# First two weight blocks side by side, row squares on ScalarE, chunk inverses by outer products, layer-norm sums kept during the convolution

## The chip, the cores and the metric

One Trainium2 chip, one of its cores, one launch. The metric is the device time of the program in microseconds (us), median of the runs shown. In the rows PE is TensorE's matmul, PEld its weight load, DVE is VectorE, ACT is ScalarE, POOL is GpSimd, SP is SyncE (here it only issues DMAs).

## What is computed

A hybrid layer on x of 256 rows by 4096 columns, all float32. The reference, cut:

```python
h = rms_norm(x, norm_pre_g)                     # x * rsqrt(mean(x*x, -1) + 1e-6) * g
proj = einsum('btd,dc->btc', h, w_in)           # 4096 x 14528 weights
rwkv_in, g_rwkv, glu_v, glu_g, g_conv = split(proj, ...)
xs = rwkv_in + (prev_row(rwkv_in) - rwkv_in) * mu_shift
r, k, v, w_low, a_low = split(xs, ...)          # decay and rate from the two low-rank parts
y = rwkv7_recurrence(r, decay, k_h, v, kk, a)   # 32 heads of 64, 256 steps
y_rwkv = (group_norm(y) * g + b + bonus) * silu(g_rwkv)
u = glu_v * sigmoid(glu_g)
c = causal depthwise conv(u, 31 taps) + conv_b  # 2048 channels
c = silu(layer_norm(c))                         # over the 2048 channels of a row
y_conv = (c @ w_pw2 + b_pw2) * silu(g_conv)
out = concat(y_rwkv, y_conv) @ w_out            # 4096 x 4096
return x + rms_norm(out, norm_post_g)
```

## The kernel before

**Blocks and slots.** The matrix products are cut into 41 blocks: 29 of `w_in` (one for each 512 output columns; the first r block and the low-rank columns make two blocks of 352), 4 of `w_pw2`, 8 of `w_out`. A block has 32 k steps (16 for `w_pw2`) of 128 rows of the weights. A k step is here called a slot; there are 1248. The weights stream from HBM in chunks of two slots (tile `wr`, 4 buffers, 512 KB each for a 512-wide block), issued by SP. Products are made from float32 split into a high and a low part: ScalarE copies `wr` to `wh` (`w_hi`), VectorE subtracts to `wl` (`w_lo`), 5 buffers of each, and a slot is 6 matmuls (`mm`): for each of two halves of 128 rows of x, `wh` by `lh`, `wl` by `lh`, `wh` by `ll` into a PSUM tile `acc` (4 buffers, two for each block). ScalarE's `wh` runs 4 slots ahead of PE, VectorE's `wl` 3.

**The head.** In the first block every slot also splits x: `x_load` fetches a transposed piece of x with the norm's factor as its last column (4 k steps a piece, 514 KB, into tiles `c_ar`, `c_q`, `c_bkt`, `c_uv`), `x_hi` makes `lh` on ScalarE and `x_lo` makes `ll` on VectorE. For the norm, `x_sq` squares each piece on GpSimd and adds it up there (tiles `t_bk`, `c_y`, 15 instructions of 128x1024 in all); `job_rstd` sums over the partitions with 8 small matmuls, takes the root and the reciprocal. Nothing of a block's result is evicted before this `rstd` is there, since the eviction scales by it. The blocks come in the order k, r (352), r rest with low-rank (352), v, gg, gv, then five blocks (k, r, v, gg, gv) for each further quarter of the channels.

**Side work.** Everything else is cut into generators (`job_...`) in lanes. At each slot `side.step` takes one step of each lane, as long as the costs booked for VectorE and ScalarE stay under those of PE; a step that yields 0 may be followed by the next at once. The order on PE, VectorE and ScalarE is that of the program. `job_prep` makes, for 4 heads at a time (8 units), the keys, decays and the masked products `qp` (64 small matmuls in two steps of 32, called `tp<-c_ar,t_bk` in the rows); `job_inv` inverts 32x32 triangular blocks of two units on VectorE (4 times; 31 steps, each a multiply and a reduction, on tiles `t_x`, `c_y`, `c_sq`); `job_chain` runs the recurrence over 8 chunks of 32 rows; `job_conv` makes the 31 taps on VectorE and writes the result to HBM; `job_ln` reads it back (tile `c_c`), sums over channels with five reductions of 128x1024 (line 783), subtracts the mean, squares on ScalarE, sums again with five reductions (line 800), scales, applies SiLU. `job_gate`, `job_mixr`, `job_mixc` build the input of the last product.

All instructions recorded through the helper `Meter` have its line, L90; SP's weight loads are L1107 and L1111.

Of the kernel before, what the change touches and what calls it, by code (L numbers as in the profile page):

```python
# [34 lines left out]
HI_LEAD, LO_LEAD = 4, 3  # L35
MANUAL = {mybir.EngineType.PE, mybir.EngineType.DVE, mybir.EngineType.Activation}
# [139 lines left out]
def hybrid(ctx: ExitStack, tc, a, out):  # L176
# [123 lines left out]

    def x_sq(i):
        xr = st["xr", i][:, :, 0:T]
        if i == 0:
            st["sa"] = rw["pool"].tile([P, 4, T], F32, name="c_y", bufs=1)
            nc.gpsimd.tensor_tensor(out=st["sa"], in0=xr, in1=xr, op=ALU.mult)
        else:
            q = rw["pool"].tile([P, 4, T], F32, name="t_bk", bufs=1)
            nc.gpsimd.tensor_tensor(out=q, in0=xr, in1=xr, op=ALU.mult)
            nc.gpsimd.tensor_tensor(out=st["sa"], in0=st["sa"], in1=q, op=ALU.add)

    def job_rstd():
# [6 lines left out]
        s1 = one.tile([P, 2], F32, name="s1")  # L318
# [109 lines left out]
    def job_prep(u):  # L428
# [112 lines left out]
        for c in range(NCH):  # L541
            for q, h in DIAG:
                pe.matmul(qp[h][HS[q ^ h], c, :], bk[HS[h], c, q, :], ar[HS[h], q * 8 + c, :], start=True, stop=True)
            if c % 4 == 3:
                for q in range(2 if c == 3 else 0):
                    vec.scalar_tensor_tensor(out=bq[:, q * T:(q + 1) * T], in0=rsv[:, q, :], scalar=par("r_k", u * 2 + q),
                                             in1=kh[:, q * T:(q + 1) * T], op0=ALU.mult, op1=ALU.mult)
                yield
# [35 lines left out]
    def job_inv(pr):  # L584
# [14 lines left out]
        vec.memset(nt.rearrange("p n k j -> p n (k j)")[:, :, 0:CH * CH:CH + 1], -1.0)  # L599
        yield 0  # L600
# [138 lines left out]
    def job_conv(j, u):  # L739
        for half in range(2):  # L740
            yield from tp_wait()
            tp = tp_get([P, 2, T])
            transposes(tp, u, half)
            if half:
                pt_put()
            yield
            ups = []
            for q in range(2):
                up = cvp.tile([P, CK - 1 + T], F32, name="up", bufs=3)
                vec.memset(up[:, 0:CK - 1], 0.0)  # L750
                act(out=up[:, CK - 1:], in_=tp[:, q, :], func=AF.Copy)
                ups.append(up)
            tp_put()
            yield
            c0 = j * 4 + half * 2
            c = cvp.tile([P, 2, T], F32, name="cw", bufs=2)
            for q in range(2):
                ct = c0 + q
                vec.tensor_scalar(out=c[:, q, :], in0=ups[q][:, 0:T], scalar1=par("conv_w", ct * CK), scalar2=par("conv_b", ct),
                                  op0=ALU.mult, op1=ALU.add)  # L760
            yield 0
            for k in range(1, CK):
                for q in range(2):
                    ct = c0 + q
                    vec.scalar_tensor_tensor(out=c[:, q, :], in0=ups[q][:, k:k + T], scalar=par("conv_w", ct * CK + k),
                                             in1=c[:, q, :], op0=ALU.mult, op1=ALU.add)
                    yield 0
            nc.gpsimd.dma_start(out=c_dr[j, :, half], in_=c.rearrange("p q t -> p (q t)"))

    def job_ln():  # L770
# [5 lines left out]
        for _ in range(6):  # L776
            yield
        s = cp.tile([P, T], F32, name="ln_s", bufs=1)
        s4 = cp.tile([P, 4, T], F32, name="ln_t", bufs=2)
        for b in range(4):  # L780
            vec.tensor_reduce(out=s4[:, b, :], in_=c[:, 4 * b:4 * b + 4, :].rearrange("p c t -> p t c"), axis=AX.X, op=ALU.add)
            yield 0
        vec.tensor_reduce(out=s, in_=s4.rearrange("p c t -> p t c"), axis=AX.X, op=ALU.add)
        for _ in range(3):
            yield
        yield from tp_wait()
        m = tp_get([P, T])
        pe.matmul(m, cs("mean"), s, start=True, stop=True)
# [8 lines left out]
        for b in range(4):  # L797
# [204 lines left out]
    ss2 = one.tile([P, 2, NB], F32, name="ss2")  # L1002
# [62 lines left out]
    for g in range(4):  # L1065
        for kind in "krv":
# [18 lines left out]
    for bi, b in enumerate(blocks):
        for k0 in range(0, b["nk"], KC):
            for kk in range(KC):
                slots.append((bi, k0 + kk, len(chunks), kk))
            chunks.append((bi, k0))
# [61 lines left out]
    with tc.manual_schedule(engines=MANUAL):  # L1151
# [107 lines left out]
```

## Time and profile before

| | |
|---|---|
| Time, median of 3 runs (lowest, highest) | 1880.1 us (1877.75, 1880.76) |
| The profiled execution: time, span | 1882.28 us, 1880.5 us |
| PE, PEld busy, share of the span | 98%, 80% |
| DVE, ACT, POOL busy | 75%, 54%, 8% |
| granted clock, mean | 0.995 |
| HBM read, written | 348.38 MB, 12.58 MB |
| Chain that ended last, by engine | PE 89%, DVE 7%, issue 2%, ACT 1%, DMA 1% |

The span is the stretch from the program's first instruction to its last; 1.8 us of the time lie around it. Busy time on PE counts matmuls that overlap in the array (one of 512 columns takes 387 to 395 ns, the next starts 227 ns later), so a full row of nines in the slices hides short idle stretches: these are read from the timeline, where each row has in brackets how long its engine was idle before it and what ended that.

### The profile page before, as it was taken

What the parts mean: (1) busy time and instruction counts of PE and PEld (TensorE: products, weight loads), DVE (VectorE), ACT (ScalarE), POOL (GpSimd) and SP (SyncE); (2) the same over time, 40 slices, a digit from 0 to 9 for tenths busy, and PEclk for the clock granted to TensorE, in tenths of its full rate; (3) what the DMA queues carried; (4) which work ended last, traced back from release to release, by engine and by line L of the source; (5) the groups of instructions that cost most, each with busy time, mean ns of one, the idle gap of its engine ahead of it and who ended that gap; (6) DMA issues with size and microseconds to landing.
All of it is one profiled execution on the core that took longest, in us unless ns stands there. A gap on an engine that the chain in (4) does not pass through costs nothing.

```text
span 1880.5 us, 31312 instructions
## 1 busy us (share of the span) xinstructions
PE 1850.0 (98%) x11585; PEld 1497.2 (80%) x11585; DVE 1415.1 (75%) x2623; ACT 1019.1 (54%) x1770; POOL 153.4 (8%) x233
## 2 busy tenths in 40 slices
PE   6999999999999999999999999999999999999997
PEld 4898888877788877888777888777888888888886
DVE  8755769997879997798996989956887655555555
ACT  4555665545565564565464565444566544445553
POOL 5200001020001020001020000110010000000000
PEclk8999999999999999999999999999999999999999
DMA  6676557664657664656664667755766766666665
GB/s 214 182 204 192 175 175 206 188 197 130 188 178 199 192 189 132 196 179 193 184 186 135 198 182 219 215 172 161 254 226 241 262 197 198 198 199 201 193 201 190
DMA packets 192713, 363.02 MB, mean 193 GB/s; under 512 B 14256, under 2 KB 31792, under 8 KB 192304
## 3 DMA queue, kind: packets, MB, share of 16 engines
q1 hardware_dynamic: 181200, 331.12, 58.1%
q0 software_dynamic: 11360, 29.90, 5.3%
q8 instruction: 91, 1.49, 0.3%
q14 instruction: 62, 0.51, 0.1%
HBM read 348.38 MB, written 12.58 MB: 192 GB/s over the span
## 4 chain that ended last, share of the span: by engine, by line
PE 89%; DVE 7%; issue 2%; ACT 1%; DMA 1%; SPq 0%; DVEq 0%; ACTq 0%; POOLq 0%
PE acc L90 82%; PE tp L90 4%; DVE wl L90 3%; PE pz L90 3%; DVE c_sq L90 1%; DVE cw L90 1%; DVE ll L90 1%; ACT wh L90 0%; DVE ln_t L90 0%; DMA wr<-in_w_in 0%; DVE t_x L90 0%; DVE chl L90 0%; DMA t_bk<-in_w_lora_up 0%; DVE c_c L90 0%; ACT L90 0%
## 5 line engine op out<-in xcount | busy, mean ns | idle before, releaser
L90 ACT ACTIVATE wh<-wr 128x512 fp32r<-128x512 f32 (+1 forms) x1243 | 771.0, 624 | 679.9 <-PE acc L90 428.3
L90 DVE TENSOR_TENSOR wl<-wr,wh 128x512 fp32r<-128x512 f32 (+1 forms) x1243 | 847.9, 692 | 292.9 <-ACT wh L90 290.1
L90 PE MATMUL acc<-wl,lh 128*128 128x512 f32 (+1 forms) x2358 | 915.5, 388 | 17.1 <-DVE wl L90 16.8
L90 PE MATMUL acc<-wh,lh 128*128 128x512 f32 (+1 forms) x2358 | 930.9, 395 | 1.5 <-ACT wh L90 1.5
L90 PE MATMUL acc<-wh,ll 128*128 128x512 f32 (+1 forms) x2358 | 913.1, 387 | 0.0
L90 PEld LDWEIGHTS acc<-wl,lh 128*128 128x128 f32 x2358 | 444.0, 188 | 108.3 <-DVE wl L90 27.3
L90 PEld LDWEIGHTS acc<-wh,lh 128*128 128x128 f32 x2358 | 443.6, 188 | 94.3 <-ACT wh L90 2.7
L90 PEld LDWEIGHTS acc<-wh,ll 128*128 128x128 f32 x2358 | 443.8, 188 | 88.9
L90 DVE SCALAR_TENSOR_TENSOR cw<-up,pv,cw 128x256 f32<-128x256 f32 x480 | 217.9, 482 | 6.2 <-DMA c_y<-n_dr 5.3
L90 PE MATMUL acc<-wh,chl 128*128 128x512 f32 x256 | 82.5, 397 | 0.0
L90 DVE TENSOR_TENSOR c_sq<-t_x,c_y 128x4 f32<-128x4 f32 (+30 forms) x124 | 63.7, 514 | 0.1
L556 POOL DMA_DIRECT2D n_dr<-c_q x32 | 18.7, 590 | 528.8 <-DVE c_q L90 483.4
L90 DVE TENSOR_SCALAR c_uv<-pz 32x256 f32<-32x256 f32 x32 | 13.6, 426 | 61.5 <-ACT c_uv L90 61.3
L90 PEld LDWEIGHTS acc<-wh,chl 128*128 128x128 f32 x256 | 48.1, 188 | 11.2
L90 ACT ACT_TABLE_LOAD x39 | 50.0, 1283 | 1.4 <-PEq L1231 0.7
L90 PE MATMUL acc<-wl,chl 128*128 128x512 f32 x128 | 50.5, 395 | 0.0
L90 DVE TENSOR_REDUCE t_x<-c_sq 128x2 f32<-128x4 f32 (+30 forms) x124 | 43.5, 351 | 0.1
L90 ACT ACTIVATE c_ry<-pz 128x256 f32<-128x256 f32 x32 | 12.3, 385 | 45.7 <-PE pz L90 43.2
L618 POOL DMA_DIRECT2D c_x<-x_dr x64 | 34.7, 551 | 16.3 <-DMA x_dr<-t_x 12.5
L90 ACT ACTIVATE pt<-acc,rstd 128x512 f32<-128x512 f32 (+3 forms) x52 | 33.8, 654 | 1.6 <-PE acc L90 1.1
L90 DVE TENSOR_TENSOR c_y<-pz,c_ry 32x256 f32<-32x256 f32 (+1 forms) x48 | 20.4, 424 | 18.4 <-PE pz L90 18.0
L90 PEld LDWEIGHTS pz<-c_uv,c_q 32*64 32x64 f32 (+1 forms) x1024 | 19.7, 124 | 14.4 <-issue 12.5
(173 smaller groups left out, 940.1 us busy)
## 6 DMA issues: line engine op xcount, KB each, us to landing
wr<-in_w_in SPq DMA_DIRECT2D x431, 512.0 KB, 3.7
wr<-in_w_out SPq DMA_DIRECT2D x128, 512.0 KB, 4.6
wr<-in_w_pw SPq DMA_DIRECT2D x32, 512.0 KB, 4.8
wr<-in_w_in SPq DMA_DIRECT2D x16, 352.0 KB, 3.5
c_y<-n_dr POOLq DMA_DIRECT2D x16, 256.0 KB, 7.6
out<-chl SPq DMA_DIRECT2D x16, 256.0 KB, 2.2
wr<-in_w_in SPq DMA_DIRECT2D x16, 192.0 KB, 2.7
wr<-in_w_in SPq DMA_DIRECT2D x16, 160.0 KB, 2.4
```

The costliest lines, as they stand in the source:

```text
L90: return f(*args, **kw)
L556: nc.gpsimd.dma_start(out=n_dr[u, y].rearrange("(h g) k j -> k h g j", h=2), in_=qs[y * CH:(y + 1) * CH, :, 1 - x::2, x * CH:(x + 1) * CH])
L618: nc.gpsimd.dma_start(out=xt[y * CH:(y + 1) * CH, un, h * 4:h * 4 + 4], in_=x_dr[2 * pr + un, y ^ (2 * h), h * 4:h * 4 + 4].rearrange("g i ...
```

## The change

Four edits.

1. **Head.** The first two blocks, now k and v, run side by side: two slots of k, two of v, and so on, up to the last four k steps; those come first for k, then for v. Each piece of x now serves four slots of weights in place of two. `rstd` is needed from the end of k.
2. **Row squares.** x is fetched a second time, row by row (`x_rows`, 8 pieces of 128x1024, 512 KB, by SP), and squared and summed on ScalarE with an accumulating activation (`x_sq`); VectorE adds the 4 parts of a row. The GpSimd instructions and the small matmuls are gone.
3. **Inverses and preparation.** `job_inv` takes 31 outer-product steps (multiply, subtract) in place of 31 steps of multiply and reduce, with the longest row first and fewer elements in all; the -1 on the diagonal is no longer set. `job_prep` issues its 64 `qp` matmuls in one step.
4. **Layer norm.** `job_conv` adds its finished channels into `csum` (15 additions of 128x256); `job_ln` waits 4 steps in place of 6 and starts at the mean; the sum of squares is made by additions of 128x1024 in place of reductions.

```diff
+APART = 4
+X_EVERY = 8
...
+    def x_rows(i):
+        t = rw["pool"].tile([P, D // 4], F32, name=("c_y", "t_bk")[i % 2], bufs=1)
+        nc.sync.dma_start(out=t, in_=xk_v[:, i // 4, (i % 4) * (D // 4):(i % 4 + 1) * (D // 4)])
+        st["xs", i] = t
+
     def x_sq(i):
-        xr = st["xr", i][:, :, 0:T]
-        if i == 0:
-            st["sa"] = rw["pool"].tile([P, 4, T], F32, name="c_y", bufs=1)
-            nc.gpsimd.tensor_tensor(out=st["sa"], in0=xr, in1=xr, op=ALU.mult)
-        else:
-            q = rw["pool"].tile([P, 4, T], F32, name="t_bk", bufs=1)
-            nc.gpsimd.tensor_tensor(out=q, in0=xr, in1=xr, op=ALU.mult)
-            nc.gpsimd.tensor_tensor(out=st["sa"], in0=st["sa"], in1=q, op=ALU.add)
+        t = st["xs", i]
+        act(out=t, in_=t, func=AF.Square, accum_out=ss2[:, i // 4, i % 4:i % 4 + 1])
 
     def job_rstd():
-        yield from tp_wait()
-        s = tp_get([P, 2, 2])
-        for tt in range(2):
-            for j in range(4):
-                pe.matmul(s[:, tt, :], st["sa"][:, j, tt * P:(tt + 1) * P], cs("mean")[:, 0:2], start=(j == 0), stop=(j == 3))
-        yield
         s1 = one.tile([P, 2], F32, name="s1")
-        act(out=s1, in_=s[:, :, 0], func=AF.Sqrt, scale=W / D, bias=eps[:, 0:1])
-        tp_put()
+        vec.tensor_reduce(out=s1, in_=ss2[:, :, 0:4], axis=AX.X, op=ALU.add)
+        yield
+        act(out=s1, in_=s1, func=AF.Sqrt, scale=1.0 / D, bias=eps[:, 0:1])
         yield
...
-            if c % 4 == 3:
-                for q in range(2 if c == 3 else 0):
-                    vec.scalar_tensor_tensor(out=bq[:, q * T:(q + 1) * T], ...)
-                yield
+        for q in range(2):
+            vec.scalar_tensor_tensor(out=bq[:, q * T:(q + 1) * T], ...)
+        yield
...
-        for j in range(1, CH):
-            l = (j + 3) // 4 if j % 4 == 0 else j // 4 + 1
+        for k in range(CH - 1):
+
+            l, m = k // 4 + 1, CH - 1 - k
             tm = rp.tile([P, 2, 8, CH], F32, name="c_sq", bufs=1)
-            vec.tensor_tensor(out=tm[:, :, 0:l, 0:j + 1], in0=xi[:, :, 0:l, 0:j + 1],
-                              in1=nt[:, :, 0:j + 1, j].unsqueeze(2).broadcast_to([P, 2, l, j + 1]), op=ALU.mult)
+            vec.tensor_tensor(out=tm[:, :, 0:l, 0:m], in0=xi[:, :, 0:l, k:k + 1].broadcast_to([P, 2, l, m]),
+                              in1=nt[:, :, k:k + 1, k + 1:].broadcast_to([P, 2, l, m]), op=ALU.mult)
             yield 0
-            vec.tensor_reduce(out=xi[:, :, 0:l, j], in_=tm[:, :, 0:l, 0:j + 1], axis=AX.X, op=ALU.add, negate=True)
+            vec.tensor_tensor(out=xi[:, :, 0:l, k + 1:], in0=xi[:, :, 0:l, k + 1:], in1=tm[:, :, 0:l, 0:m], op=ALU.subtract)
             yield 0
...
+            if c0 == 0:
+                vec.tensor_tensor(out=csum, in0=c[:, 0, :], in1=c[:, 1, :], op=ALU.add)
+            else:
+                for q in range(2):
+                    vec.tensor_tensor(out=csum, in0=csum, in1=c[:, q, :], op=ALU.add)
...
-        for kind in "krv":
+        for kind in "kvr" if g == 0 else "krv":
...
+    head = [(bi, k0) for k0 in range(0, NK - APART, KC) for bi in range(2)]
+    head += [(bi, k0) for bi in range(2) for k0 in range(NK - APART, NK, KC)]
...
-        x_load(1)
         load(2)
         load(3)
-        x_load(2)
+        x_load(1)
         load(4)
...
-                if s < 28 and s % 4 == 0:
-                    x_load(s // 4 + 3) if s // 4 + 3 < 8 else None
+                if s % X_EVERY == 0 and s // X_EVERY + 2 < 8:
+                    x_load(s // X_EVERY + 2)
                 load(i + RL)
-            if bi == 0 and k % 4 == 2 and k > 2:
-                x_sq(k // 4)
+            if s % 6 == 0 and 1 <= s // 6 <= 8:
+                x_rows(s // 6 - 1)
+            if s % 6 == 5 and 2 <= s // 6 <= 9:
+                x_sq(s // 6 - 2)
...
-            if bi == 1 and k >= 4:
+            if bi == 2:
                 side.drain(lambda: "rstd" not in st)
             side.step()
-            if evict is not None and (bi != 1 or "rstd" in st):
+            if evict is not None and "rstd" in st:
```

The order of instructions that results, at three places. GpSimd's queue at the start, before; `c_y` and `t_bk` hold the squares, `c_ar` to `c_uv` the pieces of x:

```order
L590 DMA t_x<-in_cst 128x512
L305 ISA
L305 TENSOR_TENSOR c_y<-c_ar 128x1024
L308 TENSOR_TENSOR t_bk<-c_ar 128x1024
L309 TENSOR_TENSOR c_y<-c_y,t_bk 128x1024
L308 TENSOR_TENSOR t_bk<-c_q 128x1024
L309 TENSOR_TENSOR c_y<-c_y,t_bk 128x1024
```

and now:

```order
L1236 UNCONDITIONAL_BRANCH
L588 DMA t_x<-in_cst 128x512
L430 DMA t_bk<-in_w_lora_up 96x256
L431 DMA t_bk<-in_a_lora_up 96x256
L554 DMA n_dr<-c_q 32x8x32 x4
```

All 15 arithmetic instructions have left GpSimd; only DMA issues stay on it.

ScalarE at the end of the first statistics, before (`s` is the root of the mean square, `wh` of 352 columns belongs to the r block):

```order
L90 ACTIVATE wh<-wr 128x512
L90 ACTIVATE wh<-wr 128x352 x4
L90 ACTIVATE s_626<-tp,eps 128x2
L90 ACTIVATE wh<-wr 128x352
L90 ACTIVATE pt<-acc,rstd 128x512
```

and now:

```order
L92 ACTIVATE wh<-wr 128x512 x4
L92 ACTIVATE t_bk,ss_94<-t_bk 128x1024
L92 ACTIVATE wh<-wr 128x512
L92 ACTIVATE s_919<-s_919,eps 128x2
L92 ACTIVATE wh<-wr 128x352
L92 ACTIVATE pt<-acc,rstd 128x512
L92 ACTIVATE wh<-wr 128x352
L92 ACTIVATE pt<-acc,rstd 128x512
```

The last row square, the root and the two evictions of the first block now stand between the last `wh` of the second block and the first ones of the r block, where the root stood behind four of the r block's `wh`.

PE in the preparation of the first unit, before (`acc` rows belong to a block of weights):

```order
L90 MATMUL acc<-wh,ll 128x512
L90 MATMUL tp<-c_ar,t_bk 64x64 x16
L90 MATMUL acc<-wh,lh 128x512
L90 MATMUL acc<-wl,lh 128x512
L90 MATMUL acc<-wh,ll 128x512
L90 MATMUL acc<-wh,lh 128x512
L90 MATMUL acc<-wl,lh 128x512
L90 MATMUL acc<-wh,ll 128x512
L90 MATMUL tp<-c_ar,t_bk 64x64 x16
```

and now:

```order
L92 MATMUL acc<-wl,lh 128x512
L92 MATMUL acc<-wh,ll 128x512
L92 MATMUL tp<-c_ar,t_bk 64x64 x32
L92 MATMUL acc<-wh,lh 128x512
L92 MATMUL acc<-wl,lh 128x512
```

Two pieces with one slot between them have become one piece (a program row of 16 is 32 matmul rows of the trace, since a float32 matmul runs in two passes).

## Rows read from the trace of the kernel before

**Rows 1.** Busy time by stretch: us, then PE, PEld, DVE, ACT, POOL (instructions), PEclk, DMA share, GB/s.

```profile
0.00:26.00 26.00, 14.28 (x40) 7.35 (x40) 19.58 (x16) 12.08 (x23) 17.00 (x12) 0.87 0.64 212
26.00:75.00 49.00, 41.82 (x172) 33.55 (x173) 43.78 (x57) 24.29 (x47) 19.95 (x10) 0.93 0.65 208
75.00:200.00 125.00, 125.00 (x686) 114.36 (x686) 69.58 (x128) 73.39 (x140) 0.00 (x0) 1.00 0.65 188
```

**Rows 2.** Waits of PE from 75 to 1875 us: total us, times, longest.

```profile
PE acc L90 <- DVE wl L90: 0.6, 2, 0.5
```

**Rows 3.** Chain that ended last: start us, us, what.

```profile
153.22 35.41 PE acc L90 x156
```

**Rows 4.** Timeline of PE, 10 to 76 us: start us, us, what [idle before <-releaser].

```profile
10.46 0.51 PE L90 MATMUL acc<-wh,lh 128*128 128x512 f32 x1
...
16.56 0.50 PE L90 MATMUL acc<-wl,lh 128*128 128x512 f32 x1 [3.16 <-DVE wl L90]
...
41.75 0.79 PE L90 MATMUL acc<-wl,lh 128*128 128x512 f32 x1 [3.12 <-DVE wl L90]
...
57.38 0.50 PE L90 MATMUL acc<-wl,lh 128*128 128x512 f32 x1 [2.88 <-DVE wl L90]
...
73.88 1.84 PE L90 MATMUL tp<-cst,c_y 128*128 128x2 f32 x16
75.58 0.41 PE L90 MATMUL acc<-wh,lh 128*128 128x352 f32 x1
```

**Rows 5.** Timeline of DVE, 28 to 37 us.

```profile
28.01 0.47 DVE L90 SCALAR_TENSOR_TENSOR ll<-c_q,lh 128x256 fp32r<-128x256 f32 x1
28.40 0.68 DVE L90 TENSOR_TENSOR wl<-wr,wh 128x512 fp32r<-128x512 f32 x1
...
32.00 2.11 DVE L90 SCALAR_TENSOR_TENSOR ll<-c_q,lh 128x256 fp32r<-128x256 f32 x1
34.03 2.88 DVE L90 TENSOR_TENSOR wl<-wr,wh 128x512 fp32r<-128x512 f32 x1
```

**Rows 6.** Timeline of POOL, 23 to 34 us.

```profile
23.12 2.41 POOL L309 TENSOR_TENSOR c_y<-c_y,t_bk 128x1024 f32<-128x1024 f32 x1
...
31.50 2.33 POOL L308 TENSOR_TENSOR t_bk<-c_bkt 128x1024 f32<-128x1024 f32 x1 [5.97 <-DMA c_bkt<-in_xT]
```

**Rows 7.** DMA from 1.5 to 16.5 us: rate in 40 slices; one issue group, us to landing.

```profile
GB/s 36 200 208 180 371 281 303 334 320 342 296 274 331 336 336 361 320 282 342 345 378 413 396 402 407 388 404 377 375 356 356 364 361 391 372 364 372 351 329 192
...
c_q<-in_xT SPq DMA_DIRECT2D x2, 514.0 KB, 9.5
```

**Rows 8.** Waits of SP's DMA queue, 0 to 75 us.

```profile
SPq L1111 <- DVE ll L90: 40.9, 10, 9.6
```

**Rows 9.** Timeline of PE around two pieces of preparation work.

```profile
230.56 0.39 PE L90 MATMUL acc<-wh,ll 128*128 128x512 f32 x1
...
231.50 0.50 PE L90 MATMUL acc<-wh,lh 128*128 128x512 f32 x1
...
242.27 0.39 PE L90 MATMUL acc<-wh,ll 128*128 128x512 f32 x1
...
243.68 0.50 PE L90 MATMUL acc<-wh,lh 128*128 128x512 f32 x1
```

**Rows 10.** Groups: xcount | busy us, mean ns of one | idle before.

```profile
L90 DVE TENSOR_TENSOR c_sq<-t_x,c_y 128x4 f32<-128x4 f32 (+30 forms) x124 | 63.7, 514 | 0.1
...
L90 DVE TENSOR_REDUCE t_x<-c_sq 128x2 f32<-128x4 f32 (+30 forms) x124 | 43.5, 351 | 0.1
...
L90 ACT ACTIVATE pt<-acc,rstd 128x512 f32<-128x512 f32 (+3 forms) x52 | 33.8, 654 | 1.6 <-PE acc L90 1.1
...
L90 ACT ACTIVATE ln_q<-c_c 128x1024 f32<-128x1024 f32 x4 | 4.2, 1058 | 2.7 <-DVE ln_t L90 2.7
...
L90 ACT ACTIVATION_READ_ACCUMULATOR tp<-acc 128x1 f32 x16 | 3.0, 189 | 0.0
```

**Rows 11.** Tile c_c: landing of its DMA issues.

```profile
DMA to landing us min/median/max: 7.3/9.8/11.7
```

More of the change, by code (lines that the diff above doesn't have):

```diff
@@ L213, in hybrid @@
     rstd = one.tile([P, 2], F32, name="rstd")
+    ss2 = one.tile([P, 2, D // BN], F32, name="ss2")
     lowh = one.tile([LORA, 2, T], F32R, name="lowh")
@@ L216, in hybrid @@
     bones = one.tile([P, P], F32R, name="bones")
+    csum = one.tile([P, T], F32, name="csum")
     ident = cs("ident")
@@ L299, in x_lo @@
                                  in1=st["lh"][:, kt, :].bitcast(F32), op0=ALU.mult, op1=ALU.subtract)
+    def x_rows(i):
+        t = rw["pool"].tile([P, D // 4], F32, name=("c_y", "t_bk")[i % 2], bufs=1)
+        nc.sync.dma_start(out=t, in_=xk_v[:, i // 4, (i % 4) * (D // 4):(i % 4 + 1) * (D // 4)])
+        st["xs", i] = t
     def x_sq(i):
-        xr = st["xr", i][:, :, 0:T]
-        if i == 0:
-            st["sa"] = rw["pool"].tile([P, 4, T], F32, name="c_y", bufs=1)
-            nc.gpsimd.tensor_tensor(out=st["sa"], in0=xr, in1=xr, op=ALU.mult)
-        else:
-            q = rw["pool"].tile([P, 4, T], F32, name="t_bk", bufs=1)
-            nc.gpsimd.tensor_tensor(out=q, in0=xr, in1=xr, op=ALU.mult)
-            nc.gpsimd.tensor_tensor(out=st["sa"], in0=st["sa"], in1=q, op=ALU.add)
-    def job_rstd():
-        yield from tp_wait()
-        s = tp_get([P, 2, 2])
-        for tt in range(2):
-            for j in range(4):
-                pe.matmul(s[:, tt, :], st["sa"][:, j, tt * P:(tt + 1) * P], cs("mean")[:, 0:2], start=(j == 0), stop=(j == 3))
+        t = st["xs", i]
+        act(out=t, in_=t, func=AF.Square, accum_out=ss2[:, i // 4, i % 4:i % 4 + 1])
+    def job_rstd():
+        s1 = one.tile([P, 2], F32, name="s1")
+        vec.tensor_reduce(out=s1, in_=ss2[:, :, 0:4], axis=AX.X, op=ALU.add)
         yield
-        s1 = one.tile([P, 2], F32, name="s1")
-        act(out=s1, in_=s[:, :, 0], func=AF.Sqrt, scale=W / D, bias=eps[:, 0:1])
-        tp_put()
+        act(out=s1, in_=s1, func=AF.Sqrt, scale=1.0 / D, bias=eps[:, 0:1])
         yield
@@ L775, in job_ln @@
             nc.gpsimd.dma_start(out=c[:, 4 * b:4 * b + 4, :].rearrange("p c t -> p (c t)"), in_=c_dr[b].rearrange("p h x -> p (h x)"))
-        for _ in range(6):
-            yield
[L778 to L784, printed above, removed]
+        for _ in range(4):
             yield
@@ L787, in job_ln @@
         m = tp_get([P, T])
-        pe.matmul(m, cs("mean"), s, start=True, stop=True)
+        pe.matmul(m, cs("mean"), csum, start=True, stop=True)
         yield
@@ L796, in job_ln @@
         s4 = cp.tile([P, 4, T], F32, name="ln_t", bufs=2)
-        for b in range(4):
+        act(out=s4, in_=c[:, 0:4, :], func=AF.Square)
+        for b in range(1, 4):
             sq = cp.tile([P, 4, T], F32, name="ln_q", bufs=1)
@@ L800, in job_ln @@
             yield
-            vec.tensor_reduce(out=s4[:, b, :], in_=sq.rearrange("p c t -> p t c"), axis=AX.X, op=ALU.add)
+            vec.tensor_tensor(out=s4, in0=s4, in1=sq, op=ALU.add)
             yield
         cv["sq"] = True
-        vec.tensor_reduce(out=s, in_=s4.rearrange("p c t -> p t c"), axis=AX.X, op=ALU.add)
-        for _ in range(3):
+        vec.tensor_tensor(out=s4[:, 0:2, :], in0=s4[:, 0:2, :], in1=s4[:, 2:4, :], op=ALU.add)
+        vec.tensor_tensor(out=csum, in0=s4[:, 0, :], in1=s4[:, 1, :], op=ALU.add)
+        for _ in range(2):
             yield
@@ L808, in job_ln @@
         m = tp_get([P, T])
-        pe.matmul(m, cs("mean"), s, start=True, stop=True)
+        pe.matmul(m, cs("mean"), csum, start=True, stop=True)
         yield
@@ L1001, in hybrid @@
     NB = D // BN
-    ss2 = one.tile([P, 2, NB], F32, name="ss2")
     def pre_out(j):
@@ L1084, in hybrid @@
     slots = []
[L1085 to L1089, printed above, removed]
+    head = [(bi, k0) for k0 in range(0, NK - APART, KC) for bi in range(2)]
+    head += [(bi, k0) for bi in range(2) for k0 in range(NK - APART, NK, KC)]
+    for bi, k0 in head + [(bi, k0) for bi, b in enumerate(blocks[2:], 2) for k0 in range(0, b["nk"], KC)]:
+        for kk in range(KC):
+            slots.append((bi, k0 + kk, len(chunks), kk))
+        chunks.append((bi, k0))
     st["lh"] = xp.tile([P, NK, T], F32R, name="lh")
@@ L1171, in hybrid @@
                 w_lo(s - (HL - LL))
-        x_sq(0)
         acc = None
@@ L1190, in hybrid @@
                     b["pre"]()
-                acc = [ps_acc.tile([P, b["n"]], F32, name="acc") for _ in range(2)]
+                b["acc"] = [ps_acc.tile([P, b["n"]], F32, name="acc") for _ in range(2)]
+            acc = b["acc"]
             if b["lhs"] is CHL:
@@ L1214, in hybrid @@
                 if evict is not None:
+                    side.drain(lambda: "rstd" not in st)
                     while next(evict, "end") != "end":
```

6 lines of the change are left out of this document (2 added, 4 removed).

## The prediction

> **What bounds the kernel.** I began with busy time by stretch [rows 1]. From 75 us on PE's busy time fills the stretch at a granted clock of 1.00 (the upper level, 2.4 GHz); before that it does not: 14.3 of the first 26 us and 41.8 of the next 49, with the clock at 0.87 and 0.93. Next the waits of PE: from 75 to 1875 us it lost 0.6 us to VectorE's `wl` [rows 2]. So behind the first block only fewer or shorter instructions on PE can change the time, and VectorE, however busy, costs nothing there. The chain gives PE's undisturbed pace: 156 matmuls, which are 26 slots, in 35.41 us, so 1.362 us a slot [rows 3].
>
> The timeline of the head shows what the first block loses. Slot 2 starts at 10.46 us; then PE stands still for about 3 us at a time, at 16.56, 41.75 and 57.38 us among others, each time for VectorE's `wl`; a row of 0.79 us is a matmul at the lower clock (1.2 GHz) behind such a stop. The 16 matmuls of the row statistics follow at 73.88, and the second block starts at 75.58 us [rows 4]. At full pace its 30 slots from 10.46 would have ended at 51.3, so some 24 us are lost. VectorE's own timeline says why: the same `ll` takes 0.47 us at 28.01 and 2.11 at 32.00, the same `wl` 0.68 and 2.88 [rows 5]. The long ones lie where GpSimd computes its squares: its sum at 23.12 ends at 25.53, the next square starts at 31.50 [rows 6], and VectorE is fast in between. Busy time agrees: GpSimd worked 17.0 us of the first 26 and 20.0 of the next 49, and not at all from 75 to 200 [rows 1]. A slow pair (2.11 and 2.88, some overlap) needs about 4.9 us where PE needs 1.36, so VectorE sets the pace while GpSimd computes.
>
> **The change, part by part, against the profiled execution (span 1880.5, time 1882.3, which is 2.2 above the median of 1880.1; I carry the difference over to the median).**
>
> *Head.* To compare like with like I take the end of two 512-wide blocks. Before: 75.58 plus 32 slots of 1.362 (43.6) is 119.2; this holds the old row-statistics matmuls, which are removed. After: the DMAs up to slot 2 stand in the same order, so slot 2 starts at 10.46 again; its `wl` can be ready only about 0.68 after `wh` [rows 5] where the first matmul takes 0.23, a stop of 0.4; then 62 slots of 1.362 (84.4) end at 95.3. That needs VectorE at 0.47 for every second slot and 0.68 for each, 0.9 a slot, which fits. Gain **23.9 us**. Without GpSimd's share a single block would have gained nearly as much; side by side each piece of x serves twice the matmuls.
>
> *What must keep up.* ScalarE gets 8 squares: 1.06 us for 128x1024 and 0.19 for reading the accumulator [rows 10], 10 us in 87, beside some 0.9 us of copies a slot. A square stands 11 slots (15 us) behind its DMA's issue; the slowest landing of a half-megabyte piece of x in the crowded start was 9.5 us [rows 7]. I take 0; each microsecond by which a square came late would be one for every `wh` behind it on ScalarE. SP issues 8 more DMAs among the weight loads; one whose tile is free holds the queue for about half a microsecond, and in the old head that queue stood 40.9 us behind `ll` [rows 8], so it has room. `rstd` now comes after the last square; then the root and two evictions of 0.65 [rows 10], under 3 us, must be done before the r block takes their `acc` tiles. The last four slots of v, 5.4 us of PE, cover it. Without this cover PE would stand up to 3 us.
>
> *DMA.* Between slots 0 and 49 SP issues 25 weight chunks, 6 pieces of x, 8 row pieces and 0.76 MB of parameters: 13.1 + 3.2 + 4.2 + 0.8 = 21.2 MB, in 49 slots or 66.7 us, so 318 GB/s. In the second half of the stretch from 1.5 to 16.5 us, with the queue full, 19 slices of 20 lie between 329 and 413 [rows 7]. The other end: 188 GB/s at a share of 0.65 [rows 1] is 290 GB/s at 1.00; there the 21.2 MB take 73.1 us, 6.4 more than PE, less what the four buffers hold. I take 0, since the full-queue row is the same traffic at the same place, and keep +6 for the range. The Trainium skill (DMA: Bandwidth & Descriptors, Specifications) gives about 358 GB/s for one core's share of HBM: by it the 21.2 MB would take 59 us and cost nothing, while the full-queue slices go above that figure.
>
> *Preparation.* A piece of 32 rows of small matmuls costs PE 0.94 us from the matmul before to the one behind (230.56 to 231.50), one of 64 costs 1.41 (242.27 to 243.68) [rows 9]. Two of the first less the 0.23 that the further matmul would take anyway are 1.65, against 1.41, and the high-part matmul behind every piece itself runs 0.1 longer: 0.35 saved in each of 8 units, **2.8 us**. The two VectorE products that stood between the halves are done elsewhere in its slack.
>
> *Inverses.* Now 107.2 us of VectorE for 124 multiplies and 124 reductions [rows 10]. After: 124 multiplies and 124 subtractions on about half the elements (3120 against 5856 for each pair of units); at most twice the old 63.7, so between 60 less and 20 more on VectorE. PE waited 0.6 us for it in 1800; 0 on PE, with that 0.6 as the most it can give. If the cover went, it would show as `wl` late beside the inverses.
>
> *Layer norm.* Ten reductions of 128x1024 go; 15 additions of 128x256 in the convolution and five larger ones come. All on VectorE under PE: 0. One wait is new: the mean's subtraction follows the reading of `c_c` by five slots (6.8 us), and that lands after 7.3 to 11.7 us [rows 11]. VectorE may stand up to 4.9 us; its lead of three slots (4.1 us) hides all but 0.8. I take 0.
>
> Sum: 23.9 + 2.8 = 26.7 less, a span of 1853.8, a time of 1855.6; on the median 1880.1 - 26.7 = **1853.4 us**.
>
> **Rivals.** *DMA just short, or the clock down for a while.* If the head moves 290 GB/s it loses up to 6.4; a fall of the clock like those behind the old stops, for 4 to 8 us of PE's work, costs 2 to 4. For it: 318 needed is close to what the queue has shown. Against: the full-queue slices. Time about 1859, up to 1866.
>
> *The slow VectorE rows are not GpSimd's doing* but go with the landing of x itself. Then the head keeps its stops and only the small pieces (2.8) and the old row-statistics matmuls (1.7, from 73.88 to 75.58 [rows 4]) are gained: 1875.6. Against it: long and short rows part exactly at GpSimd's start and end.
>
> *The squares hold ScalarE.* If the row pieces land two microseconds after their square's turn, eight times, 16 of the gain go: 1869. For it: they queue behind weights in a DMA system near its limit. Against: 15 us of lead.
>
> *Slower.* The head becomes bound by DMA altogether. Its first 26 us moved 212 GB/s [rows 1]; were that what the chip gives to this traffic, 21.2 MB would take 100 us, 33 more than PE: the head would end at 128.6 in place of 119.2, and with the 2.8 the time is 1886.7. It decides from where the head ends at 122.0, a rate of 227 GB/s. Against it: in that stretch the queue was waiting for buffers that VectorE freed late [rows 8], not for the transfers.
>
> **How the numbers follow.** Forecast as summed, 1849 to 1858: 0.69. DMA or clock, 1857 to 1866: 0.17. Slow rows stay: 0.05. Squares hold ScalarE: 0.05. Slower: 0.04. The range 1848 to 1866 takes the first two. 0.2% (3.8 us) is about what a measurement of this kernel can tell from no change; the rivals that gain lie below that bound, so faster 0.95, same 0.01, slower 0.04.
>
> **What would show it.** Right: GpSimd has no arithmetic; VectorE's `ll` and `wl` stay near 0.47 and 0.68 from the start; no stop of PE over half a microsecond between 12 and 95 us; the r block's first matmul near 95; a clock above 0.95 in the first 75 us; 8 pieces of 64 rows near 1.4 us; PE's time from the r block on unchanged but for these. Wrong: stops of PE that end with a DMA of `wr`, `ll` near 2 us without GpSimd, squares that start on a landing, a first r matmul after 100 us, or `wl` late behind `c_c`.

## The result and the profile after

The changed kernel takes **1850.25 us**, the median of 4 runs (1849.65 to 1850.36), against 1879.57 for the kernel before on the same chip: a ratio of 0.984, 95% interval 0.983 to 0.986, or 29.3 us less. The forecast was 1853.4, which is 26.7 less than the 1880.1 it started from. In the three later sets of runs the kernel before took 1877.56 to 1878.72, so by the set the gain is 27.3 to 29.3. The profiled execution took 1850.36 us with a span of 1848.5.

The page of the changed kernel, its first part (busy time, share, instructions) and the first line of the chain by engine:

```profile
PE 1835.3 (99%) x11569; PEld 1495.3 (81%) x11569; DVE 1345.9 (73%) x2630; ACT 1024.4 (55%) x1785; POOL 118.3 (6%) x218
...
PE 98%; DVE 1%; DMA 0%; ACT 0%; SPq 0%; issue 0%; DVEq 0%
```

Busy time by stretch in the changed kernel, with the columns of [rows 1]:

```profile
0.00:26.00 26.00, 23.38 (x88) 16.38 (x89) 14.95 (x31) 15.67 (x29) 0.87 (x5) 1.00 0.95 329
26.00:75.00 49.00, 49.00 (x218) 40.57 (x217) 32.59 (x59) 35.76 (x68) 0.00 (x0) 1.00 0.93 319
75.00:200.00 125.00, 125.00 (x685) 114.39 (x684) 72.48 (x134) 81.75 (x157) 1.04 (x2) 1.00 0.67 189
```

PE now fills the second stretch (49.00 of 49.00), the granted clock is 1.00, the upper level, from the start, and GpSimd computes nothing any more (the 0.87 us are four memsets and a DMA issue). The price is in the last two columns: the DMA share of the head went from 0.64 to 0.95.

PE's timeline in the changed kernel: slot 2, the first 352-wide matmul (the r block) and the first matmul of the fifth block (slot 128).

```profile
10.23 0.50 PE L92 MATMUL acc<-wh,lh 128*128 128x512 f32 x1 [0.92 <-ACT wh L92]
10.96 0.49 PE L92 MATMUL acc<-wl,lh 128*128 128x512 f32 x1 [0.23 <-DVE wl L92]
...
95.20 0.32 PE L92 MATMUL acc<-wh,lh 128*128 128x352 f32 x1
...
158.41 0.39 PE L92 MATMUL acc<-wh,lh 128*128 128x512 f32 x1
```

The same place in the kernel before, and below it, for each kernel, the first matmul of slot 928, where the product with `w_pw2` begins. First before:

```profile
183.03 0.39 PE L90 MATMUL acc<-wh,lh 128*128 128x512 f32 x1
...
1427.43 0.40 PE L90 MATMUL acc<-wh,chl 128*128 128x512 f32 x1
```

and after:

```profile
1395.71 0.40 PE L92 MATMUL acc<-wh,chl 128*128 128x512 f32 x1
```

This places the gain. After 128 slots, the same work in both orders, the changed kernel is 183.03 - 158.41 = 24.6 us ahead. From slot 128 to 928 it gains 31.7 - 24.6 = 7.1 more, and from there to the end only 0.3 (the spans differ by 32.0). So there are two gains: the head, and the middle (slots 128 to 928), where the chunk preparation, the inverses and the layer norm run under PE. Both are differences between one execution of each kernel; the part on the prediction says how much of them belongs to the execution.

VectorE's timeline in the head reads like the fast pair of [rows 5] now, though x arrives at the same time:

```profile
23.98 0.69 DVE L92 TENSOR_TENSOR wl<-wr,wh 128x512 fp32r<-128x512 f32 x1 [0.67 <-ACT wh L92]
24.59 0.47 DVE L92 SCALAR_TENSOR_TENSOR ll<-c_q,lh 128x256 fp32r<-128x256 f32 x1
```

The groups of the inverses, and of the mean's subtraction behind `c_c`, against [rows 10]:

```profile
L92 DVE TENSOR_TENSOR c_sq<-t_x,c_y 128x120 f32<-128x120 f32 (+24 forms) x124 | 31.8, 257 | 4.0 <-DMA c_y<-n_dr 3.9
L92 DVE TENSOR_TENSOR t_x<-t_x,c_sq 128x120 f32<-128x120 f32 (+24 forms) x124 | 31.7, 256 | 0.1
...
L92 DVE TENSOR_TENSOR c_c<-c_c,tp 128x1024 f32<-128x1024 f32 x4 | 4.8, 1214 | 1.8 <-DMA c_c<-c_dr 1.8
```

The inverses take 63.5 us of VectorE instead of 107.2. The new wait behind `c_c` exists: VectorE stood 1.8 us for that DMA.

### The profile page after: what moved, and what is told of

It is laid out like the page before. It is cut to its first block, busy times and chain, and to the rows that moved or that the text cites. A ratio compares the mean times of both kernels' runs of the same rounds, so it can differ in the third digit from the quotient of the medians.

```text
span 1848.5 us, 31244 instructions
## 1 busy us (share of the span) xinstructions
PE 1835.3 (99%) x11569; PEld 1495.3 (81%) x11569; DVE 1345.9 (73%) x2630; ACT 1024.4 (55%) x1785; POOL 118.3 (6%) x218
## 4 chain that ended last, share of the span: by engine, by line
PE 98%; DVE 1%; DMA 0%; ACT 0%; SPq 0%; issue 0%; DVEq 0%
PE acc L92 92%; PE tp L92 4%; PE pz L92 3%; DMA wr<-in_w_in 0%; DVE chl L92 0%; DVE wl L92 0%; DVE t_pi L92 0%; ACT L92 0%; SPq L291 0%; ACT wh L92 0%; DVE c_y L92 0%; SPq L1104 0%; ACT tp L92 0%; DVEq L1236 0%; ACT t_sw L92 0%
## 5 line engine op out<-in xcount | busy, mean ns | idle before, releaser
L92 DVE TENSOR_TENSOR wl<-wr,wh 128x512 fp32r<-128x512 f32 (+1 forms) x1243 | 831.5, 677 | 339.9 <-ACT wh L92 335.4
L92 PEld LDWEIGHTS acc<-wh,chl 128*128 128x128 f32 x256 | 48.1, 188 | 11.1
L554 POOL DMA_DIRECT2D n_dr<-c_q x32 | 18.6, 589 | 489.0 <-DVE c_q L92 438.3
L92 DVE TENSOR_TENSOR c_sq<-t_x,c_y 128x120 f32<-128x120 f32 (+24 forms) x124 | 31.8, 257 | 4.0 <-DMA c_y<-n_dr 3.9
L92 DVE TENSOR_TENSOR t_x<-t_x,c_sq 128x120 f32<-128x120 f32 (+24 forms) x124 | 31.7, 256 | 0.1
L92 DVE RECIPROCAL t<-t 128x128 f32<-128x128 f32 x32 | 29.8, 940 | 0.3
```

Of the source, the lines that this page charges most:

```text
L92: return f(*args, **kw)
L554: nc.gpsimd.dma_start(out=n_dr[u, y].rearrange("(h g) k j -> k h g j", h=2), in_=qs[y * CH:(y + 1) * CH, :, 1 - x::2, x * CH:(x + 1) * CH])
```

## Experiments

All kernels were timed beside the kernel before, whose median was 1877.56 in the first set (7 runs), 1878.72 in the second (7) and 1878.04 in the third (21). The changed kernel was timed again in the second set: 1850.04 (1849.59 to 1850.54). A loss is counted from 1850.25 in the first set and from 1850.04 in the second.

**The head: which part gives the 24 us?** My theory was that GpSimd's squares slow VectorE; the rivals were a loss that comes with x's landing, a DMA limit, and squares that hold ScalarE.

*Squares alone moved, blocks still one after the other* (on the kernel before):

```diff
 def x_sq(i):
-    xr = st["xr", i][:, :, 0:T]
...
-        nc.gpsimd.tensor_tensor(out=q, in0=xr, in1=xr, op=ALU.mult)
-        nc.gpsimd.tensor_tensor(out=st["sa"], in0=st["sa"], in1=q, op=ALU.add)
+    act(out=t, in_=t, func=AF.Square, accum_out=ss2[:, i // 4, i % 4:i % 4 + 1])
...
+            if s % 3 == 0 and s // 3 < 8:
+                x_rows(s // 3)
+            if s % 3 == 2 and 2 <= s // 3 <= 9:
+                x_sq(s // 3 - 2)
```

> The kernel before with one edit: x read a second time by rows and its squares made on ScalarE (8 pieces, one every 3 slots), nothing of them on GpSimd; blocks one after the other, as before. If the head was lost to GpSimd's arithmetic alone, VectorE's ll and wl stay at 0.47 and 0.68 and the second block starts near 52 in place of 75.6 us: about 1857. If the second reading of x needs the blocks side by side to be carried, the first block is bound by DMA: 8.4 MB of weights, 8.4 of x and some 2.5 run ahead in one block at 320 to 370 GB/s take 52 to 60 us, so the second block starts at 58 to 66: 1863 to 1871, with stops of PE that end with a DMA. If VectorE is slowed by the landing of x, its rows stay at 2 to 2.9 us and the time stays near 1875.

Measured: 1858.99 (1858.63 to 1859.22), ratio 0.990 [0.988, 0.991]; 18.6 us from this part alone, where the whole change gives 27.3 against this set's kernel before. Its stretches, then its second block and its slot 128:

```profile
0.00:26.00 26.00, 23.40 (x89) 15.99 (x90) 15.64 (x33) 16.87 (x33) 0.87 (x5) 1.00 0.97 340
26.00:75.00 49.00, 48.22 (x249) 41.79 (x248) 33.07 (x69) 38.23 (x82) 1.04 (x2) 1.00 0.89 298
```

```profile
53.90 0.32 PE L90 MATMUL acc<-wh,lh 128*128 128x352 f32 x1
...
161.26 0.39 PE L90 MATMUL acc<-wh,lh 128*128 128x512 f32 x1
```

The second block starts at 53.90 instead of 75.58 [rows 4], at a DMA share of 0.97, and PE is busy 48.22 of the 49 us. So even one block after the other the transfers carried the head.

*The GpSimd instructions put back into the changed kernel, their result unused:*

```diff
+    def idle_sq(i):
+        xr = st["xr", i][:, :, 0:T]
+        q = rw["pool"].tile([P, 4, T], F32, name="c_bv", bufs=1)
+        nc.gpsimd.tensor_tensor(out=q, in0=xr, in1=xr, op=ALU.mult)
+        if i:
+            nc.gpsimd.tensor_tensor(out=q, in0=q, in1=xr, op=ALU.add)
...
+            if s % 8 == 2 and s // 8 < 8:
+                idle_sq(s // 8)
```

> The changed kernel with the 15 GpSimd instructions of 128x1024 put back in the head, their result used by nobody. If GpSimd's arithmetic is what slows VectorE, ll and wl beside them take 2.1 and 2.8 us again, PE stops for about 3 us at a time and 15 to 22 us of the gain are lost: 1865 to 1872. If VectorE's slow rows came from the landing of x, nothing changes: 1850.

Measured: 1856.50 (1854.14 to 1857.65), ratio 0.988 [0.987, 0.990]; 6.3 us lost, well under the 15 to 22 that I had written down. The profiled execution is the fastest of the four: 1854.14, 3.8 above that of the changed kernel. Timelines of its GpSimd, VectorE and PE:

```profile
16.39 2.26 POOL L320 TENSOR_TENSOR c_bv<-c_bv,c_ar 128x1024 f32<-128x1024 f32 x1
18.73 2.23 POOL L318 TENSOR_TENSOR c_bv<-c_q 128x1024 f32<-128x1024 f32 x1
21.03 2.23 POOL L320 TENSOR_TENSOR c_bv<-c_bv,c_q 128x1024 f32<-128x1024 f32 x1
30.93 1.89 POOL L318 TENSOR_TENSOR c_bv<-c_q 128x1024 f32<-128x1024 f32 x1 [7.67 <-DMA c_q<-in_xT]
32.90 2.19 POOL L320 TENSOR_TENSOR c_bv<-c_bv,c_q 128x1024 f32<-128x1024 f32 x1
```

```profile
16.51 2.69 DVE L92 TENSOR_TENSOR wl<-wr,wh 128x512 fp32r<-128x512 f32 x1
19.12 2.11 DVE L92 SCALAR_TENSOR_TENSOR ll<-c_ar,lh 128x256 fp32r<-128x256 f32 x1
```

```profile
23.87 0.50 PE L92 MATMUL acc<-wl,lh 128*128 128x512 f32 x1 [2.94 <-DVE wl L92]
```

The long `ll` and `wl` are back, in the changed kernel, with data that nobody reads. That is the cause; x's landing is not. What I had mis-sized is when it costs: the first burst has four instructions without a gap (13.72 to 23.26) and ends in one stop of PE, 2.94 us. The later ones have two (30.93 to 35.09, 4.2 us), and no stop follows: PE is busy 49.00 us of the stretch from 26 to 75. That VectorE catches up in between, since side by side it needs 0.9 of every 1.36 us, is argued. The other three executions lost 5.9 to 7.4 us at a mean granted clock of 0.997 in place of 0.998; no trace shows where.

*The old statistics on GpSimd whole, blocks side by side* (the changed kernel with the old `x_sq` and `job_rstd`, and in the loop):

```diff
-            if s % 6 == 0 and 1 <= s // 6 <= 8:
-                x_rows(s // 6 - 1)
-            if s % 6 == 5 and 2 <= s // 6 <= 9:
-                x_sq(s // 6 - 2)
+            if s % 8 == 2 and s // 8 < 8:
+                x_sq(s // 8)
```

> The changed kernel with the old row statistics: squares and sums on GpSimd from the transposed pieces, no second reading, the blocks still side by side. If GpSimd's arithmetic is the cause, 36 us of it in the head cost about as much as before, spread over two blocks: ll and wl at 2.1 and 2.8 us beside it, 15 to 24 us lost, 1865 to 1875. If placing the blocks side by side is what gained, by halving what VectorE must do for x in a slot, it stays within 5 us of 1850.

Measured: 1863.08 (1861.34 to 1866.37), ratio 0.992 [0.991, 0.994]; 12.8 us lost, under the 15 to 24 expected. PE's waits in the first 100 us (total, times, longest), and its slot 128:

```profile
PE acc L92 <- DVE wl L92: 8.3, 8, 3.1
```

```profile
171.90 0.39 PE L92 MATMUL acc<-wh,lh 128*128 128x512 f32 x1
```

Here GpSimd computes almost without a gap from 52.09 to 67.7 us, and stops of PE come back there. Slot 128 starts 13.5 us later than in the changed kernel: 8.3 are these waits, the old row-statistics matmuls (1.7) stand in the head again, and the granted clock is 0.97 and 0.94 in the stretches to 26 and 75 us. With this run the head is a table of four starts of slot 128: 183.0 as it was; 171.9 with only the blocks side by side; 161.3 with only the squares moved; 158.4 with both. Moving the squares gives 21.8 alone, going side by side 11.1 alone, and only 2.9 once the squares are gone. Each start is that of one execution, and the one of the kernel before was long in its head: in two other runs with the same head (new inverses alone and one-step qp alone, below) slot 128 starts at 180.21 and 180.72, by which the first two gains are 2.3 to 2.8 smaller.

*Changed kernel without the second reading of x and the squares:*

```diff
-            if s % 6 == 0 and 1 <= s // 6 <= 8:
-                x_rows(s // 6 - 1)
-            if s % 6 == 5 and 2 <= s // 6 <= 9:
-                x_sq(s // 6 - 2)
+            if s == 5:
+                vec.memset(ss2[:, :, 0:4], 1024.0)
```

> The changed kernel without the row statistics (the sums of squares are constants; neither the second reading of x nor the 8 squares are done). If the second reading costs nothing since PE is the bound in the head, the first r matmul stays at 95.2 us and the time at 1850 within 0.7. If DMA at a share of 0.93 to 0.95 holds PE back somewhere, or ScalarE does, up to 1.5 us are gained.

Measured: 1851.49 (1850.70 to 1852.40), ratio 0.986 [0.984, 0.988]: no gain, and 1.2 us above the changed kernel where I had allowed 0.7. The r block begins at 95.91 instead of 95.20, but slot 2 at 10.97 instead of 10.23: between the two lie 84.94 us here and 84.97 in the changed kernel. The 4.2 MB read again and 10 us of ScalarE cost nothing, as I took them.

**The middle: where do 7 us come from, when I had 2.8?** Each of the three edits was undone in the changed kernel, and two were done alone on the kernel before; the layer norm alone was not run. Beside the time I read each run's middle, from the start of slot 128 to that of slot 928. In four executions with the changed kernel's order there (two of the changed kernel, the idle GpSimd instructions, the old statistics) it is 1237.3 to 1237.4 us.

*Old inverses in the changed kernel* (the memset and the loop of 15 multiplies and reductions in place of the outer products):

```diff
+        vec.memset(nt.rearrange("p n k j -> p n (k j)")[:, :, 0:CH * CH:CH + 1], -1.0)
...
+            vec.tensor_reduce(out=xi[:, :, 0:l, j], in_=tm[:, :, 0:l, 0:j + 1], axis=AX.X, op=ALU.add, negate=True)
-            vec.tensor_tensor(out=xi[:, :, 0:l, k + 1:], in0=xi[:, :, 0:l, k + 1:], in1=tm[:, :, 0:l, 0:m], op=ALU.subtract)
```

> The changed kernel with the old inverses (multiply and reduce). From slot 128 to slot 928 the change gained 7.1 us where I had 2.8; the rest lies in rows of PE in which the first low-part matmul came late. If the old inverses held wl up (107 us of VectorE in place of 63.5), 3 to 4 us are lost: 1853 to 1854, with wl among the waits of the weight load again. If the gain came from fewer pieces of small matmuls alone, it loses under 1 us (203 pieces in place of 200).

Measured: 1854.87 (1853.95 to 1856.53), ratio 0.987 [0.986, 0.989]; 4.8 us lost; the middle is 1241.5, 4.2 longer. The waits behind the head tell where, once the weight-load engine is looked at beside PE. Its row in the kernel before, and in this run:

```profile
PEld acc L90 <- DVE wl L90: 7.0, 19, 0.9
```

```profile
PEld acc L92 <- DVE wl L92: 6.2, 18, 1.0
```

The changed kernel has no such row in that stretch. PE's own row in the kernel before showed 0.6 [rows 2]; the `wl` that is late holds up its weight load first, and the time is booked there. Of the 18 waits of this run 17 lie at its fourth inverse (1119 to 1176 us). Of the 19 of the kernel before ten (3.0 us) lie at the third inverse, six (2.1) at the fourth and three (1.9) beside the old layer norm's reductions, so 5.1 of the 7.0 us belong to the inverses.

What such a wait costs can be read from the first experiment (squares alone moved). Behind the head its PE, VectorE and ScalarE have the instructions of the kernel before in the same order, yet its middle is 1404.09 - 161.26 = 1242.8 us, where the kernel before has 1427.43 - 183.03 = 1244.4. The two keep step within 0.2 us up to slot 565; then the third inverse begins. The kernel before from 860 to 945 us, its weight load and the VectorE row ahead of that inverse:

```profile
PEld acc L90 <- DVE wl L90: 3.0, 10, 0.5
```

```profile
866.60 0.44 DVE L90 SCALAR_TENSOR_TENSOR cw<-up,pv,cw 128x256 f32<-128x256 f32 x1 [3.73 <-DMA c_y<-n_dr]
```

and in the first experiment the same VectorE row, and its slot 928:

```profile
841.48 0.44 DVE L90 SCALAR_TENSOR_TENSOR cw<-up,pv,cw 128x256 f32<-128x256 f32 x1 [0.24 <-DVE wl L90]
```

```profile
1404.09 0.40 PE L90 MATMUL acc<-wh,chl 128*128 128x512 f32 x1
```

There the weight load has none of the ten waits. So 3.0 us of them cost PE 1.6, while PE's own row for `wl` in the middle is 0.6 us in the kernel before and 0.7 in the experiment. They came after VectorE had stood 3.73 us for the landing of the triangular blocks (`c_y<-n_dr`); that this landing used up its lead is read from this one pair. With the new inverses VectorE stood 3.9 to 7.0 us for the same landing in the four executions named above, whose middles agree within 0.1 us.

*The qp products in two steps again:*

```diff
+            if c % 4 == 3:
+                for q in range(2 if c == 3 else 0):
...
+                yield
```

> The changed kernel with the masked products in two steps of 32 again. By the prediction 0.35 us in each of 8 units: 2.8 lost, 1853.1. By the count of pieces (205 in place of 200, since other pieces meet) at 0.25 to 0.35 each, 1.3 to 1.8: 1851.8. If pieces cost nothing, 1850.3.

Measured: 1853.87 (1853.69 to 1854.10), ratio 0.987 [0.985, 0.988]; 3.8 us lost, against 1.3 to 2.8 expected; the middle is 1241.2, 3.9 longer. PE's pieces of small matmuls behave as read: one of 64 in the changed kernel takes 217.42 to 218.83, the 1.41 of [rows 9].

```profile
217.42 0.39 PE L92 MATMUL acc<-wh,ll 128*128 128x512 f32 x1
217.74 1.16 PE L92 MATMUL tp<-c_ar,t_bk 64*64 64x64 f32 x64
218.83 0.50 PE L92 MATMUL acc<-wh,lh 128*128 128x512 f32 x1
```

But a wait of the recurrent chain grew with it. The weight-load engine's waits for `c_uv`, changed kernel and this run:

```profile
PEld pz L92 <- DVE c_uv L92: 1.2, 2, 0.8
```

```profile
PEld pz L92 <- DVE c_uv L92: 3.5, 6, 0.8
```

*The old layer norm:*

```diff
-            if c0 == 0:
-                vec.tensor_tensor(out=csum, in0=c[:, 0, :], in1=c[:, 1, :], op=ALU.add)
...
+            vec.tensor_reduce(out=s4[:, b, :], in_=c[:, 4 * b:4 * b + 4, :].rearrange("p c t -> p t c"), axis=AX.X, op=ALU.add)
```

> The changed kernel with the old layer norm (ten reductions of 128x1024, no sums kept in the convolution). By the prediction all of it lies under PE: 1850.3 within 0.7; 197 pieces in place of 200 could even give 0.5 to 1. If the reductions of 2 us each held wl up, 1 to 2 us are lost.

Measured: 1852.61 (1851.98 to 1853.27), ratio 0.986 [0.985, 0.988]; 2.6 us lost where I expected nothing; the middle is 1239.3, 2.0 longer. Two rows of the same view of this run:

```profile
PEld pz L92 <- DVE c_uv L92: 2.6, 4, 0.8
...
PEld acc L92 <- DVE wl L92: 1.8, 3, 0.8
```

The three waits for `wl` (1250 to 1278 us) lie beside the reductions (1240 to 1278 us). The waits for `c_uv` do not: they lie between 434 and 940 us; what differs there is that the convolution no longer makes its sums. At slot 800 (1217.45 us), ahead of the first reduction, this run is already 1.05 us behind.

The three losses add up to 11.2 us, more than the middle's whole gain of 7.1. So the parts were also done alone.

*New inverses alone, on the kernel before* (the diff of the old inverses above, backwards):

> The kernel before with the new inverses alone. If the old ones held wl up, the 7.0 us of waits of the weight load for wl behind the head go and 3 to 4.5 us are gained: about 1874 to 1876 where the kernel before has 1878.7. By the prediction, which took VectorE's work there as hidden, under 0.6.

Measured: 1877.25 (11 runs, 1876.38 to 1878.38), ratio 0.9995 [0.9987, 1.0004]: 0.8 us, not to be told from none, although the waits did fall (the three that are left lie beside the old layer norm's reductions):

```profile
PEld acc L90 <- DVE wl L90: 2.1, 3, 0.9
```

Its slots 128 and 928:

```profile
180.21 0.39 PE L90 MATMUL acc<-wh,lh 128*128 128x512 f32 x1
...
1421.77 0.40 PE L90 MATMUL acc<-wh,chl 128*128 128x512 f32 x1
```

The middle is 1241.6 us: 2.8 less than that of the kernel before, and 1.3 less than the 1242.8 of the first experiment, which has the same code there and lost nothing to the landing. The time shows less of it, since 2.2 to 2.9 us of it lie outside the span in this run and 1.75 to 1.91 in the kernel before; by the median span it is 1874.5 against 1876.2, 1.7 us less. Why the rest around the span grew no run shows.

*One-step qp alone, on the kernel before:*

> The kernel before with the masked products in one step alone (202 pieces in place of 212). By the prediction 2.8 us are gained, by the count of pieces 2.5 to 3.5: about 1875.5 to 1876.5.

Measured: 1877.98 (11 runs, 1877.24 to 1881.07), ratio 1.000 [0.999, 1.001]: nothing. Its slots 128 and 928:

```profile
180.72 0.39 PE L90 MATMUL acc<-wh,lh 128*128 128x512 f32 x1
...
1422.85 0.40 PE L90 MATMUL acc<-wh,chl 128*128 128x512 f32 x1
```

The middle is 1242.1 us, 2.3 less than that of the kernel before and 0.7 less than the first experiment's; by the median span the run is 0.6 us shorter (1875.6). For the time both expectations failed. Each edit undone costs more (4.2 and 3.9 in the middle) than it gives alone (1.3 to 2.8, and 0.7 to 2.3): the parts do not add up. Where a side piece lands among the chain's steps moves with every edit, and the waits for `c_uv` move with it (1.2, 2.6 and 3.5 us above; 1.0 in the kernel before and 2.5 in this run); that this shift is the whole of it is argued, not shown.

**Would fewer pieces still pay?** If a piece of side work has a price of its own, merging more of them must gain. The first run makes one of two in three places (the z products, the gate's and mixc's transposes), 184 pieces instead of 200; the second does so for the z products alone, 192 pieces.

```diff
-        for i in range(2):
-            yield from tp_wait()
-            z = tp_get([P, 2, T])
+        while tpn[0] > 0:
+            yield "wait"
+        zs = [tp_get([P, 2, T]) for _ in range(2)]
+        for i, z in enumerate(zs):
```

> The changed kernel with 16 pieces fewer on PE (184 in place of 200): the two low-rank products of a unit in one piece, and both halves of the transposes in the gate and in the last mix in one piece. At the 0.25 to 0.35 us that a piece cost where two were made one, 4.0 to 5.6 are gained: 1844.4 to 1846. If a piece is dear only among the very small matmuls, under 1.5 us are gained.

> The changed kernel with the two low-rank products of each unit in one piece alone (192 pieces in place of 200): half of the gain of the run with 184, 2.0 to 2.8, so 1847.2 to 1848; no change if what counts is not the number of pieces.

Measured: 1850.69 (1850.32 to 1851.40) and 1850.60 (1850.25 to 1851.31), ratios 0.986 [0.984, 0.987] and 0.986 [0.984, 0.987]: no gain. The timeline of the changed kernel around one z piece, and then of the second run around its merged piece:

```profile
184.16 0.39 PE L92 MATMUL acc<-wh,ll 128*128 128x512 f32 x1
...
185.11 0.40 PE L92 MATMUL acc<-wh,lh 128*128 128x512 f32 x1
```

```profile
183.74 0.39 PE L92 MATMUL acc<-wh,ll 128*128 128x512 f32 x1
...
185.41 0.40 PE L92 MATMUL acc<-wh,lh 128*128 128x512 f32 x1
```

One piece of 6 matmuls takes 0.95, two 1.90 less the 0.23 of the stream's own matmul counted twice, 1.67; the merged one takes 185.41 - 183.74 = 1.67. A z piece of 96x256 matmuls has no price beyond its matmuls. For the transposes only the total is known: they did not pay either. No version faster than the changed kernel came out of these runs.

The changed kernel's second timing, in the same set as the three undone edits:

> The changed kernel once more, as the measure for the three that follow: 1850.3 within 0.7.

Measured: 1850.04, ratio 0.985 [0.983, 0.986].

## Why the prediction was right, and where it was not

**Right: the head's mechanism and its end.** "62 slots of 1.362 (84.4) end at 95.3": the r block began at 95.20. GpSimd's share was the cause (the first two experiments); DMA at a share of 0.93 to 0.97 did not stop PE; the clock stayed at its upper level; the squares on ScalarE and the second reading were free (the run without them). The first 26 us moved 329 GB/s and the next 49 moved 319, where I had taken 318 as needed. The rivals "not GpSimd's doing", "squares hold ScalarE" and "bound by DMA" fell. The sentence that a single block "would have gained nearly as much" held: 21.8 of 24.6 at slot 128.

**Right at zero: the `c_c` wait.** VectorE stood 1.8 us for it, under the 4.9 bound, and PE had no row for it.

**Wrong: "0.6 as the most it can give" for the inverses.** That bound came from PE's rows alone [rows 2]. The weight-load engine had waited 7.0 us for `wl`, 5.1 of it at the inverses, and in the pair with the same order 3.0 us of such waits cost PE 1.6 while its own row did not tell them (0.6 and 0.7). The sign named for it, `wl` late beside the inverses, stood in the kernel before already. Alone the new inverses shorten the middle by 1.3 to 2.8; in the changed kernel the old ones cost 4.8.

**Wrong: the layer norm at 0.** "All on VectorE under PE" overlooked that its reductions of 2 us each delay `wl`: three waits, 1.9 us, in the kernel before. Put back they cost 2.6, of which 1.05 came ahead of the first reduction, where the side work had moved; how much the reductions alone cost is not shown.

**Mis-sized: 2.8 for the pieces.** The single piece costs what the rows said, but undone the edit lost 3.8, and alone it shortened the middle by 0.7 to 2.3, which the time does not show. A sum over parts was the wrong form for this stretch: 2.8 forecast, 7.1 measured between the profiled executions, 5.5 against the middle of the first experiment, and these runs do not divide it among the edits.

**The profiled execution of before was longer than most.** It took 1882.28 us, 2.2 above its median; "I carry the difference over to the median" took it to lie everywhere. It lies in two places. The two single edits of the middle leave the head's code alone, and their slot 128 starts at 180.21 and 180.72 instead of 183.03, so 2.3 to 2.8 us of the 24.6 belonged to that execution's head. And 1.6 of its middle came with the waits at the third inverse that the first experiment does not have.

That leaves about 22 us for the head, 5.5 for the middle and 0.3 at the end, 27.6 to 28.1, beside 27.3 to 29.3 by the medians. The forecast's 23.9 for the head was some 2 us too large, since it was taken from that execution, and its 2.8 for the middle 2.7 too small. The two errors partly cancelled, and that 1853.4 came within 3.2 us is in part luck.

## What to carry to other kernels

When an engine off the path suddenly takes four times its usual time, put its rows beside GpSimd's in the same stretch: two engines that never wait for each other in the program can still cost each other. Count a late operand on PE's weight-load row as well as on PE's own before calling a cover complete. Test edits in a packed pipeline both ways, undone and alone, and read the stretch where they act beside the time; where the two differ, quote the sum and not a share for each.

## What the runs showed of the hardware

A small VectorE instruction with one tensor input is held too. In the run with the old statistics side by side, GpSimd's and VectorE's timelines show it:

```profile
62.85 2.43 POOL L313 TENSOR_TENSOR t_bk<-c_uv 128x1024 f32<-128x1024 f32 x1 [0.88 <-DMA c_uv<-in_xT]
```

```profile
63.45 1.87 DVE L92 TENSOR_SCALAR omu<-pv 128x48 f32<-128x48 f32 x1
```

In the changed kernel `omu` takes 0.18 us. Here it ends at 65.32, with GpSimd's instruction at 65.28. The Trainium skill (SBUF — State Buffer, Who interferes with whom) says that a VectorE instruction with two SBUF inputs, or one such as tensor_scalar in a two-port mode, shares a port with a GpSimd instruction that reads SBUF, and that whichever starts second waits for the whole of the other. These rows agree, though none shows in which mode `omu` ran, and so do the `wl` of 2.69 and the `ll` of 2.11 beside the GpSimd instructions of 2.26 and 2.23 that began before them. What the price is for the kernel then hangs on the length of a burst against VectorE's lead: in the profiled run with idle GpSimd instructions 9.5 us without a gap stopped PE for 2.94, and 4.2 us stopped it not at all.
